# One decoder step on one Trainium2 core: feed-forward's first group in one 512-column matmul from inner block four, and two small products of linear attention on all 128 rows

## The chip, the core and the metric

The kernel runs on one core of a Trainium2 chip. The core has a matrix engine (TensorE, PE in the profile, with its weight loads as PEld), three engines for everything else (VectorE = DVE, ScalarE = ACT, GpSimd = POOL), and queues that issue transfers (SP's above all). TensorE writes to PSUM, eight banks of 512 fp32 columns on each of 128 partitions; the other engines read results there. The metric is device time in microseconds, the median of three runs.

## The reference

One step of a two-layer decoder: 512 prompt tokens and 8 sampled tokens, width 1024. Layer 0 mixes tokens with sliding-window attention, layer 1 with gated linear attention (GLA); behind each mixer stands a gated convolutional feed-forward of inner width 2816. Cut to what matters here:

```
def conv_ffn(x, buf, w_up, conv_w, conv_b, w_down):
    h = x @ w_up
    a, u = h[..., :D_FF], h[..., D_FF:]
    ap = concatenate([buf, a], axis=1)
    c = conv_b + sum(conv_w[j] * ap[:, j:j + T] for j in range(3))
    y = (gelu(c) * u) @ w_down
    return y, ap[:, T:]

def gla_mix(...):
    q, k, v, g = split(x @ w_in)
    log_a = log_sigmoid((x @ w_a1) @ w_a2 + b_a) / 16
    o, s_new = gla_recurrence(q, k, v, log_a, s0, chunk)
    ...
x = layer_norm(ALPHA * x + mixer(x)); x = layer_norm(ALPHA * x + conv_ffn(x))
```

All of it is float32.

## The kernel before

Tokens stand in the columns, features in the 128 rows (`P`), in eight blocks (`KD`). The 520 columns are two groups: a (256 prompt tokens) and b (256 prompt tokens and the 8 samples, 264 columns). The program is a list of units, one per block of 128 output features; each unit has one weight block of up to 1024 x 128 and runs first for group a and four or five units later for group b (`order`, with `LEADS` and `LAG`), so that a's results have time to become b's inputs. Feed-forward has 22 inner blocks j, in three parts of 6, 8 and 8 (`FF_PARTS`): for each j a gate unit (L530) and a value unit (L556), and after a part eight down units (L569) that add the part's products to x.

Precision: a weight block is split into a high part `wh` (rounded to the matmul's fp32r type, by ScalarE, L149) and a low part `wl` (what is left, by VectorE, L152); activations likewise into `xh`, `xl` (the normalised x) and `hh`, `hl` (the inner products). `product` (L155) sums, for each of a unit's k-steps, high x high, high x low and low x high in one bank: L164, L165, L166, three matmuls of 256 columns (group b: 264). The tiles of a group hold even and odd columns in two halves, and a matmul reads them in turn (`in_turn`), one column from each half.

Each matmul loads its own 128 x 128 weights. There are four accumulators (`accp`), six weight buffers (`WSLOTS`; one more in feed-forward, `EXTRA`) and two buffers for raw weights. What comes out of a gate product is copied with its two left neighbours (L540), goes through three convolution steps (L543 to L545) and GELU (L552); a value product is multiplied with it (L560) and split (L170, L171). Down products are added to x (L573, L575), or for the last part go into the layer norm.

In GLA the decay comes from a rank-16 product whose result `z` holds its rows in two halves; `gla_decay` (L633) multiplies one half, 64 rows, with `wa2` for each head and group. The samples' output (L784) gets its last term from a product with 8 rows, one per sample (`qkd`, `vsamp`). These two are plain fp32 matmuls.

Which instruction stands where on an engine is decided by the library's scheduler, which simulates the program; the engines then run their instructions in that order.

Of the kernel before, what the change touches and what calls it, by code (L numbers as in the profile page):

```python
# [11 lines left out]
F32 = mybir.dt.float32  # L12
# [8 lines left out]
P = 128  # L21
# [32 lines left out]
NSUB = 5  # L54

SPAUSE = 2
SPAUSEL = 3
# [19 lines left out]
def in_turn(rows):  # L77

    return rows.rearrange("p t j -> p j t")
# [10 lines left out]
class Net:  # L90
    def __init__(self, tc, ctx, I, O):
# [17 lines left out]
        nc.gpsimd.memset(self.ones_a, 1.0 / D)  # L109
        self.ones_c = c.tile([P, P], F32, name="ones_c")  # L110
        nc.gpsimd.memset(self.ones_c, 1.0 / P)
# [3 lines left out]
        for g in self.groups:  # L115
            s = [P, KD, g.n]
            g.x = self.act.tile(s, F32, name=f"x_{g.name}")

            s = [P, KD, 2, g.n // 2]
            g.xh = self.act.tile(s, F32R, name=f"xh_{g.name}")  # L120
# [34 lines left out]
    def product(self, g, u, rh, rl):  # L155
# [11 lines left out]
        return ps[:, :g.n]  # L167

    def split(self, hi, lo, src):
        self.nc.scalar.activation(hi, src, AF.Copy)  # L170
        self.nc.vector.tensor_tensor(lo, src, hi.bitcast(F32), op=ALU.subtract)  # L171
# [8 lines left out]
    def ln_chunk(self, g, m, ps, scaled, last=False):  # L180
# [11 lines left out]
        if m == 0:  # L192
            yield 1
            mp = self.mtile("sc")[:, :n]
            nc.tensor.matmul(mp, self.ones_c, x[:, 0], start=True, stop=True)
            sb = c("sb")
            nc.scalar.copy(sb, mp)
            sa = sb
            if not scaled:
                sa = c("sa")  # L200
                nc.scalar.activation(sa, mp, AF.Copy, scale=1.0 / ALPHA)
# [80 lines left out]
    def attn_open(self):  # L282
# [10 lines left out]
        for _ in range(WARM):  # L293
            nc.tensor.matmul(warm[:, :P], self.ones_c, self.ones_c, start=True, stop=True)
        with self.tc.manual_schedule(engines={mybir.EngineType.SP}):
# [234 lines left out]
    def ffn_gate(self, g, u, layer, j, q):  # L530
        nc, n = self.nc, g.n
        ps = self.product(g, u, g.xh, g.xl)
        w = lambda i: self.par[:, C_CW + (layer * 3 + i) * NF + j:C_CW + (layer * 3 + i) * NF + j + 1]
# [8 lines left out]
        c = t("conv")  # L542
        nc.scalar.activation(c[:, :256], ps[:, :256], AF.Identity, scale=w(2), bias=cb)  # L543
        nc.vector.scalar_tensor_tensor(c[:, :256], a[:, 1:257], w(1), c[:, :256], op0=ALU.mult, op1=ALU.add)
# [11 lines left out]
    def ffn_value(self, g, u, layer, j, q):  # L556
        nc, n = self.nc, g.n
        ps = self.product(g, u, g.xh, g.xl)
        h = self.fp.tile([P, NT - 256], F32, name="hprod", bufs=2)
        nc.vector.tensor_tensor(h[:, :n], g.gate[:, :n], ps, op=ALU.mult)  # L560
        self.split(g.hh[:, q], g.hl[:, q], parted(h[:, :n]))
# [7 lines left out]
    def ffn_down(self, g, u, layer, part, m):  # L569
        nc = self.nc  # L570
        ps = self.product(g, u, g.hh, g.hl)
        if part == 0:
# [60 lines left out]
    def gla_decay(self, g, h):  # L633
        nc, n = self.nc, g.n
        zp = self.mtile("sc")[:, :n]
        half = slice(64 * (h // 2), 64 * (h // 2) + 64)
        nc.tensor.matmul(zp, self.wa2[half, h % 2 * P:(h % 2 + 1) * P], g.z[half], start=True, stop=True)
        ba = self.par[:, C_BA + h:C_BA + h + 1]
# [122 lines left out]
    def gla_sample(self, g, h, q, k, v0, v1, ep, kraw):  # L761
# [10 lines left out]
        nc.tensor.matmul(mp[:NS, 256:257], pr, self.eps[:, 1:2], start=True, stop=True)  # L772
        vs = self.gp.tile([NS, 257], F32, name="vsamp")
        nc.vector.tensor_copy(vs, mp[:NS, :257])
        dv = self.dram.tile([NS, 256], F32, name="dv")
        nc.sync.dma_start(out=dv, in_=vs[:, :256])
        nc.vector.tensor_scalar(self.qkd.rearrange("p (j s) -> p s j", j=4)[:, 0:2],
                                self.ident[:NS, :NS].rearrange("p (t j) -> p t j", t=2), vs[:, 256:257], None, op0=ALU.mult)
        yield 1
# [209 lines left out]
def _layout(inp):  # L989
# [21 lines left out]
    a["w_a1"] = f["gla_w_a1"][0].reshape(KD, P, 16).transpose(1, 0, 2)  # L1011
    w2 = np.zeros((P, 256), np.float32)
    for i in range(2):
        w2[64 * i:64 * i + 16] = w2[64 * i + 32:64 * i + 48] = f["gla_w_a2"][0][:, 256 * i:256 * i + 256]
    a["w_a2"] = w2
# [42 lines left out]
```

## Time and profile before

| | us |
|---|---|
| median of three runs | 1170.98 (1170.62 to 1171.20) |
| the profiled execution | 1171.17 |
| its span, first to last instruction | 1169.5 |
| VectorE busy | 765.3 (65%) |
| ScalarE busy | 548.3 (47%) |
| HBM read and written | 108.54 MB and 8.47 MB |

The profile's page gives busy time by engine, the chain that ended last, and groups of instructions by line with their count, busy time, mean duration and the idle time ahead of them with what ended it. Views of the trace narrow this to a stretch, a line or a tile. In the rows, `accp<-xh_a,wh` names the tile written and the tiles read; `128*128` are the rows and columns of the weights, `128x256` the rows and columns of the moving operand. In the timeline the first number is the start and the second the duration; fp32 products show two records each (`x2`).

### The profile page before, as it was taken

The page shows a single profiled execution, that of the slowest core. Times are in us where ns is not written, and L with a number is a line of the kernel's source. Part 1 is how long each engine was busy: PE and PEld are TensorE (multiplying, and loading weights), DVE is VectorE, ACT ScalarE, POOL GpSimd, SP SyncE. Part 2 cuts the span into 40 slices and gives each one's busy share as a digit, 9 for nine tenths or more (in the row PEclk, how much of TensorE's full clock was granted, in tenths as well). Part 3 has the DMA queues.
Part 4 walks back from the last instruction along what each step waited for, and adds up shares of the span by engine and source line. Part 5 has one row for each costly group of instructions (what it writes and reads, how often), then busy time and mean ns, then how long its engine had stood idle before and what let it go on. Part 6 is the DMA issues. An engine that isn't in the chain of part 4 may idle for free.

```text
span 1169.5 us, 24320 instructions
## 1 busy us (share of the span) xinstructions
PE 1120.0 (96%) x9606; PEld 1086.6 (93%) x9606; DVE 765.3 (65%) x1575; ACT 548.3 (47%) x1192; POOL 362.5 (31%) x597
## 2 busy tenths in 40 slices
PE   8889898999999999999899999998999999999995
PEld 7888788999999999998799899898999999999995
DVE  7988869744555355468767787789645554455566
ACT  4456546533453234435545555456533453244433
POOL 5777767310111001156400100368200111011344
PEclk9999989999999999999899999999999999999998
DMA  7322022224322323233034354442323333323222
GB/s 231 114 90 74 2 79 91 83 82 127 99 100 94 106 91 109 73 125 120 26 93 124 128 189 140 142 132 73 98 86 125 104 97 94 106 92 108 74 62 73
DMA packets 48674, 118.59 MB, mean 101 GB/s; under 512 B 5768, under 2 KB 22320, under 8 KB 48560
## 3 DMA queue, kind: packets, MB, share of 16 engines
q1 hardware_dynamic: 46544, 115.41, 31.6%
q10 hardware_dynamic: 2016, 1.62, 0.4%
q8 instruction: 76, 1.25, 0.4%
q14 instruction: 38, 0.31, 0.1%
HBM read 108.54 MB, written 8.47 MB: 100 GB/s over the span
## 4 chain that ended last, share of the span: by engine, by line
PE 74%; DVE 14%; POOL 4%; issue 4%; DMA 2%; ACT 2%; SPq 0%; ACTq 0%; DVEq 0%; POOLq 0%
PE accp L165 23%; PE accp L164 23%; PE accp L166 23%; DVE wl L152 3%; DMA vb<-dv 2%; DVE qs L387 1%; POOL x_b L270 1%; POOL x_a L270 1%; DVE u L268 1%; DVE rb L338 1%; PE pv L460 1%; DVE msq L248 1%; PE sc L723 1%; DVE small L427 1%; DVE rb L336 1%
## 5 line engine op out<-in xcount | busy, mean ns | idle before, releaser
L152 DVE TENSOR_TENSOR wl<-raw,wh 128x1024 fp32r<-128x1024 f32 (+2 forms) x189 | 230.5, 1220 | 133.6 <-ACT wh L149 131.8
L149 ACT ACTIVATE wh<-raw 128x1024 fp32r<-128x1024 f32 (+1 forms) x176 | 183.2, 1041 | 216.4 <-PE accp L165 192.2
L164 PE MATMUL accp<-xh_b,wh 128*128 128x264 f32 x976 | 272.8, 280 | 2.7 <-DVE hprod L560 2.7
L164 PE MATMUL accp<-xh_a,wh 128*128 128x256 f32 x976 | 270.8, 280 | 4.2 <-DVE x_b L189 1.1
L165 PE MATMUL accp<-xl_a,wh 128*128 128x256 f32 x976 | 271.0, 279 | 3.3 <-DVE xl_a L273 2.9
L166 PE MATMUL accp<-xh_a,wl 128*128 128x256 f32 x976 | 270.8, 278 | 3.0 <-DVE wl L152 3.0
L165 PE MATMUL accp<-xl_b,wh 128*128 128x264 f32 x976 | 272.3, 279 | 0.2
L166 PE MATMUL accp<-xh_b,wl 128*128 128x264 f32 x976 | 271.6, 278 | 0.0
L164 PEld LDWEIGHTS accp<-xh_a,wh 128*128 128x128 f32 x976 | 187.4, 193 | 7.3 <-DVE x_b L189 1.6
L166 PEld LDWEIGHTS accp<-xh_a,wl 128*128 128x128 f32 x976 | 188.4, 193 | 4.9 <-DVE wl L152 4.0
L165 PEld LDWEIGHTS accp<-xl_a,wh 128*128 128x128 f32 x976 | 188.2, 193 | 5.0 <-DVE xl_a L273 3.6
L164 PEld LDWEIGHTS accp<-xh_b,wh 128*128 128x128 f32 x976 | 186.1, 191 | 4.0 <-DVE hprod L560 3.0
L165 PEld LDWEIGHTS accp<-xl_b,wh 128*128 128x128 f32 x976 | 186.1, 191 | 1.5 <-issue 0.7
L166 PEld LDWEIGHTS accp<-xh_b,wl 128*128 128x128 f32 x976 | 185.8, 190 | 0.8 <-issue 0.7
L164 PE MATMUL accp<-hh_b,wh 128*128 128x264 f32 x480 | 134.3, 280 | 3.0 <-ACT hh_b L170 3.0
L165 PE MATMUL accp<-hl_b,wh 128*128 128x264 f32 x480 | 134.6, 280 | 0.0
L166 PE MATMUL accp<-hh_b,wl 128*128 128x264 f32 x480 | 133.7, 278 | 0.0
L165 PE MATMUL accp<-hl_a,wh 128*128 128x256 f32 x480 | 132.2, 276 | 0.9 <-DVE hl_a L171 0.9
L164 PE MATMUL accp<-hh_a,wh 128*128 128x256 f32 x480 | 132.1, 278 | 0.0
L166 PE MATMUL accp<-hh_a,wl 128*128 128x256 f32 x480 | 131.9, 276 | 0.0
L164 PEld LDWEIGHTS accp<-hh_b,wh 128*128 128x128 f32 x480 | 91.7, 191 | 3.5 <-ACT hh_b L170 3.3
L165 PEld LDWEIGHTS accp<-hl_a,wh 128*128 128x128 f32 x480 | 92.0, 192 | 1.9 <-DVE hl_a L171 1.4
(306 smaller groups left out, 2052.8 us busy)
## 6 DMA issues: line engine op xcount, KB each, us to landing
raw<-in_w_up SPq DMA_DIRECT2D x88, 512.0 KB, 3.4
raw<-in_w_down SPq DMA_DIRECT2D x32, 512.0 KB, 3.5
raw<-in_w_gla SPq DMA_DIRECT2D x24, 512.0 KB, 3.4
raw<-in_w_mix_o SPq DMA_DIRECT2D x16, 512.0 KB, 3.4
raw<-in_w_down SPq DMA_DIRECT2D x16, 384.0 KB, 3.1
sgla<-in_state_gla SPq DMA_DIRECT2D x16, 256.0 KB, 2.8
vb<-dv SPq DMA_DIRECT2D x16, 256.0 KB, 3.9
out_gla_s<-sgla SPq DMA_DIRECT2D x16, 256.0 KB, 2.8
```

What stands on the lines that cost most here:

```text
L149: nc.scalar.activation(h[:, c], r[:, c], AF.Copy)
L152: nc.vector.tensor_tensor(l[:, c], r[:, c], h[:, c].bitcast(F32), op=ALU.subtract)
L164: nc.tensor.matmul(o, h[:, ks], xh, start=k == 0, stop=False)
L165: nc.tensor.matmul(o, h[:, ks], xl, start=False, stop=False)
L166: nc.tensor.matmul(o, l[:, ks], xh, start=False, stop=k == nt - 1)
L248: nc.vector.scalar_tensor_tensor(q, q, 0.5, nv, op0=ALU.mult, op1=ALU.mult)
L268: nc.vector.tensor_tensor(u, x[:, m], r, op=ALU.mult)
L270: ts = nc.gpsimd.tensor_scalar(x[:, m], u, sc(m), bi(m), op0=ALU.mult, op1=ALU.add)
L336: nc.vector.stream_shuffle(b, a, [(i + 16) % 32 for i in range(32)])
L338: nc.vector.tensor_tensor(b, b, tab[:, 1], op=ALU.mult)
L387: nc.vector.tensor_tensor(qs[oth, v], r[own, :256], qs[own, v].bitcast(F32), op=ALU.subtract)
L427: nc.vector.tensor_reduce(nm, sc[:, :, 0:P + 1], axis=AX.X, op=ALU.max, negate=True)
```

## The change

Group a's high and low parts are put side by side in one tile (`xs`, `hs`), and `xh`, `xl`, `hh`, `hl` become views of it. A new `product2` then multiplies the high weights with both parts in one matmul of 512 columns, and the low weights with the high part in one of 256, so that high x low lands in the upper half of the bank. It is used for gate and value from j = 4 (`WIDE`) on, which is the fifth block, and for the down products of parts 0 and 1. The two halves of the bank are added behind it: a gate on VectorE after the copy, a value by a ScalarE copy and a VectorE addition, a down product by a second addition to x. Group b and all other products stay as they are.

In GLA `wa2` is laid out as 128 rows per head, with zeros where the other half stands, and the samples' tiles get 128 rows, zero from row 8 on. The constant 1/128 is dropped: the layer norm's first mean uses the 1/1024 one and a scale of 8.

```
@@ __init__
+            if i == 0:
+                s = [P, KD, 2, 2, g.n // 2]
+                g.xs = self.act.tile(s, F32R, name=f"xs_{g.name}")
+                g.hs = self.act.tile(s, F32R, name=f"hs_{g.name}")
+                g.xh, g.xl = (g.xs[:, :, :, q] for q in range(2))
+                g.hh, g.hl = (g.hs[:, :, :, q] for q in range(2))
+                continue
+    def product2(self, g, u, rs, rh, rl, wide):
+        if rs is None or not wide:
+            return self.product(g, u, rh, rl), None
...
+        o = ps.rearrange("p (j t) -> p j t", t=2)
+        for k in range(nt):
+            ks = slice(k * P, (k + 1) * P)
+            last = k == nt - 1
+            both = lambda: nc.tensor.matmul(o, h[:, ks], in_turn(rs[:, k].rearrange("p t q j -> p t (q j)")), start=k == 0, stop=last)
+            low = lambda: nc.tensor.matmul(o[:, :P], l[:, ks], in_turn(rh[:, k]), start=False, stop=False)
+            for f in (low, both) if last else (both, low):
+                f()
+        return ps[:, :256], ps[:, 256:]
@@ ln_chunk
-            nc.tensor.matmul(mp, self.ones_c, x[:, 0], start=True, stop=True)
+            nc.tensor.matmul(mp, self.ones_a, x[:, 0], start=True, stop=True)
-            nc.scalar.copy(sb, mp)
+            nc.scalar.activation(sb, mp, AF.Copy, scale=float(KD))
@@ ffn_gate
-        ps = self.product(g, u, g.xh, g.xl)
+        ps, lo = self.product2(g, u, g.xs, g.xh, g.xl, j >= WIDE)
...
-        nc.scalar.activation(c[:, :256], ps[:, :256], AF.Identity, scale=w(2), bias=cb)
+        if lo is not None:
+            nc.vector.tensor_tensor(a[:, 2:2 + n], a[:, 2:2 + n], lo, op=ALU.add)
+        nc.scalar.activation(c[:, :256], ps[:, :256] if lo is None else a[:, 2:258], AF.Identity, scale=w(2), bias=cb)
@@ ffn_value
-        ps = self.product(g, u, g.xh, g.xl)
+        ps, lo = self.product2(g, u, g.xs, g.xh, g.xl, j >= WIDE)
+        if lo is not None:
+            nc.scalar.copy(h[:, :n], lo)
+            nc.vector.tensor_tensor(h[:, :n], h[:, :n], ps, op=ALU.add)
+            ps = h[:, :n]
@@ ffn_down
-        ps = self.product(g, u, g.hh, g.hl)
+        ps, lo = self.product2(g, u, g.hs, g.hh, g.hl, part < 2)
...
+        if lo is not None:
+            nc.vector.tensor_tensor(g.x[:, m], g.x[:, m], lo, op=ALU.add)
@@ gla_open, gla_decay, gla_sample
-        self.qkd = t([NS, P], "qkd")
+        self.qkd = t([P, P], "qkd")
+        self.vs = t([P, 257], "vsamp")
+        nc.gpsimd.memset(self.vs, 0.0)
-        self.wa2 = t([P, 256], "wa2")
+        self.wa2 = t([P, GH * P], "wa2")
-        half = slice(64 * (h // 2), 64 * (h // 2) + 64)
-        nc.tensor.matmul(zp, self.wa2[half, h % 2 * P:(h % 2 + 1) * P], g.z[half], start=True, stop=True)
+        nc.tensor.matmul(zp, self.wa2[:, h * P:(h + 1) * P], g.z, start=True, stop=True)
```

On TensorE, before the change, the last two k-steps of the first down product of part 0 in layer 0 (group a, six k-steps), and what follows it, a product of group b:

```order
L164 MATMUL accp<-hh_a,wh 128x256
L165 MATMUL accp<-hl_a,wh 128x256
L166 MATMUL accp<-hh_a,wl 128x256
L164 MATMUL accp<-hh_a,wh 128x256
L165 MATMUL accp<-hl_a,wh 128x256
L166 MATMUL accp<-hh_a,wl 128x256
L164 MATMUL accp<-xh_b,wh 128x264
L165 MATMUL accp<-xl_b,wh 128x264
```

And after, its last three k-steps (`hs_a` holds both parts):

```order
L191 MATMUL accp<-hs_a,wh 128x512
L192 MATMUL accp<-hs_a,wl 128x256
L191 MATMUL accp<-hs_a,wh 128x512
L192 MATMUL accp<-hs_a,wl 128x256
L173 MATMUL accp<-xh_b,wh 128x264
L174 MATMUL accp<-xl_b,wh 128x264
L175 MATMUL accp<-xh_b,wl 128x264
L192 MATMUL accp<-hs_a,wl 128x256
L173 MATMUL accp<-xh_b,wh 128x264
L174 MATMUL accp<-xl_b,wh 128x264
L175 MATMUL accp<-xh_b,wl 128x264
L191 MATMUL accp<-hs_a,wh 128x512
```

Two matmuls per k-step stand where three did. Before, the product ran in one piece; now three matmuls of the next product of group b stand ahead of each of the two of its last k-step, whose input is the last to be ready.

On VectorE, before, from a gate of group a to the end of the value that follows it, at the same place of the program (`wl` is the next weights' low part; the 8-column operation is group b's gate):

```order
L544 SCALAR_TENSOR_TENSOR conv<-aext,par,conv 128x256
L545 SCALAR_TENSOR_TENSOR conv<-aext,par,conv 128x256
L152 TENSOR_TENSOR wl<-raw,wh 128x768
L549 SCALAR_TENSOR_TENSOR conv<-aext,par,base 128x8
L544 SCALAR_TENSOR_TENSOR conv<-aext,par,conv 128x256
L545 SCALAR_TENSOR_TENSOR conv<-aext,par,conv 128x256
L560 TENSOR_TENSOR hprod<-conv,accp 128x256
L171 TENSOR_TENSOR hl_a<-hprod,hh_a 128x256
```

And after:

```order
L572 TENSOR_TENSOR aext<-aext,accp 128x256
L574 SCALAR_TENSOR_TENSOR conv<-aext,par,conv 128x256
L575 SCALAR_TENSOR_TENSOR conv<-aext,par,conv 128x256
L161 TENSOR_TENSOR wl<-raw,wh 128x768
L579 SCALAR_TENSOR_TENSOR conv<-aext,par,base 128x8
L574 SCALAR_TENSOR_TENSOR conv<-aext,par,conv 128x256
L575 SCALAR_TENSOR_TENSOR conv<-aext,par,conv 128x256
L592 TENSOR_TENSOR hprod<-hprod,accp 128x256
L594 TENSOR_TENSOR hprod<-conv,hprod 128x256
L199 TENSOR_TENSOR hs_a<-hprod,hs_a 128x2x128
```

Two additions have come in (L572, L592); the rest stands as it did.

On ScalarE, late in part 2 of a layer, a gate and a value of each group before the change (`wh` is the next weights' high part):

```order
L540 COPY aext<-accp 128x256
L543 ACTIVATE conv<-accp,par 128x256
L552 ACTIVATE conv<-conv 128x256
L149 ACTIVATE wh<-raw 128x1024
L540 COPY aext<-accp 128x264
L543 ACTIVATE conv<-accp,par 128x256
L170 ACTIVATE hh_a<-hprod 128x256
L552 ACTIVATE conv<-conv 128x264
```

And after:

```order
L568 COPY aext<-accp 128x256
L573 ACTIVATE conv<-aext,par 128x256
L158 ACTIVATE wh<-raw 128x1024
L582 ACTIVATE conv<-conv 128x256
L568 COPY aext<-accp 128x264
L573 ACTIVATE conv<-accp,par 128x256
L591 COPY hprod<-accp 128x256
L582 ACTIVATE conv<-conv 128x264
L198 ACTIVATE hs_a<-hprod 128x2x128
```

The weights' copy has moved ahead of group a's GELU (L582), and a copy of the upper half of the value's bank has come in (L591).

More of the change, by code (lines that the diff above doesn't have):

```diff
@@ L54 @@
 NSUB = 5
+WIDE = 4
 SPAUSE = 2
@@ L109, in __init__ @@
         nc.gpsimd.memset(self.ones_a, 1.0 / D)
-        self.ones_c = c.tile([P, P], F32, name="ones_c")
-        nc.gpsimd.memset(self.ones_c, 1.0 / P)
         self.eps = c.tile([P, 2], F32, name="eps")
@@ L114, in __init__ @@
         nc.gpsimd.memset(self.eps[:, 1:2], 1.0)
-        for g in self.groups:
+        for i, g in enumerate(self.groups):
             s = [P, KD, g.n]
             g.x = self.act.tile(s, F32, name=f"x_{g.name}")
+            if i == 0:
[5 more added lines that the diff above has]
+                continue
             s = [P, KD, 2, g.n // 2]
+            g.xs = g.hs = None
             g.xh = self.act.tile(s, F32R, name=f"xh_{g.name}")
@@ L167, in product @@
         return ps[:, :g.n]
+    def product2(self, g, u, rs, rh, rl, wide):
+        if rs is None or not wide:
+            return self.product(g, u, rh, rl), None
+        nc = self.nc
+        h, l = self.w[u]
+        nt = self.units[u][1]
+        ps = self.acc.tile([P, 512], F32, name="accp")
+        o = ps.rearrange("p (j t) -> p j t", t=2)
[7 more added lines that the diff above has]
+        return ps[:, :256], ps[:, 256:]
     def split(self, hi, lo, src):
@@ L200, in ln_chunk @@
                 sa = c("sa")
-                nc.scalar.activation(sa, mp, AF.Copy, scale=1.0 / ALPHA)
+                nc.scalar.activation(sa, mp, AF.Copy, scale=KD / ALPHA)
             for i in range(KD):
@@ L293, in attn_open @@
         for _ in range(WARM):
-            nc.tensor.matmul(warm[:, :P], self.ones_c, self.ones_c, start=True, stop=True)
+            nc.tensor.matmul(warm[:, :P], self.ones_a, self.ones_a, start=True, stop=True)
         with self.tc.manual_schedule(engines={mybir.EngineType.SP}):
@@ L772, in gla_sample @@
         nc.tensor.matmul(mp[:NS, 256:257], pr, self.eps[:, 1:2], start=True, stop=True)
-        vs = self.gp.tile([NS, 257], F32, name="vsamp")
-        nc.vector.tensor_copy(vs, mp[:NS, :257])
+        vs = self.vs
+        nc.vector.tensor_copy(vs[:NS], mp[:NS, :257])
         dv = self.dram.tile([NS, 256], F32, name="dv")
-        nc.sync.dma_start(out=dv, in_=vs[:, :256])
-        nc.vector.tensor_scalar(self.qkd.rearrange("p (j s) -> p s j", j=4)[:, 0:2],
-                                self.ident[:NS, :NS].rearrange("p (t j) -> p t j", t=2), vs[:, 256:257], None, op0=ALU.mult)
+        nc.sync.dma_start(out=dv, in_=vs[:NS, :256])
+        nc.vector.tensor_scalar(self.qkd[:NS].rearrange("p (j s) -> p s j", j=4)[:, 0:2],
+                                self.ident[:NS, :NS].rearrange("p (t j) -> p t j", t=2), vs[:NS, 256:257], None, op0=ALU.mult)
         yield 1
@@ L1011, in _layout @@
     a["w_a1"] = f["gla_w_a1"][0].reshape(KD, P, 16).transpose(1, 0, 2)
-    w2 = np.zeros((P, 256), np.float32)
-    for i in range(2):
-        w2[64 * i:64 * i + 16] = w2[64 * i + 32:64 * i + 48] = f["gla_w_a2"][0][:, 256 * i:256 * i + 256]
+    w2 = np.zeros((P, GH * P), np.float32)
+    for h in range(GH):
+        o = 64 * (h // 2)
+        w2[o:o + 16, h * P:(h + 1) * P] = w2[o + 32:o + 48, h * P:(h + 1) * P] = f["gla_w_a2"][0][:, h * P:(h + 1) * P]
     a["w_a2"] = w2
```

## The prediction

> **What bounds the kernel now.** I read the page first: the busy lines and the chain.
>
> ```profile
> span 1169.5 us, 24320 instructions
> PE 1120.0 (96%) x9606; PEld 1086.6 (93%) x9606; DVE 765.3 (65%) x1575; ACT 548.3 (47%) x1192; POOL 362.5 (31%) x597
> ...
> PE 74%; DVE 14%; POOL 4%; issue 4%; DMA 2%; ACT 2%; SPq 0%; ACTq 0%; DVEq 0%; POOLq 0%
> ```
>
> TensorE is busy 96% of the span and carries 74% of the chain that ends last. Such an average mixes stages, so the second view is busy time by stretches: feed-forward of layer 0 (212 to 540), the way into linear attention (540 to 575), linear attention (575 to 760), feed-forward of layer 1 (820 to 1100).
>
> ```profile
> core 0: us, PE busy (x) PEld busy (x) DVE busy (x) ACT busy (x) POOL busy (x), PEclk, DMA share, GB/s
> ...
> 212.00:465.00 253.00, 253.00 (x2259) 253.00 (x2259) 131.27 (x236) 104.59 (x186) 30.60 (x86) 1.00 0.32 101
> 465.00:540.00 75.00, 75.00 (x664) 74.78 (x663) 46.45 (x82) 32.75 (x62) 31.25 (x48) 1.00 0.34 106
> 540.00:575.00 35.00, 29.36 (x212) 25.81 (x210) 31.98 (x70) 19.13 (x37) 23.14 (x22) 0.93 0.18 61
> 575.00:760.00 185.00, 183.36 (x1497) 170.06 (x1496) 135.23 (x323) 95.38 (x247) 20.04 (x26) 0.99 0.42 132
> ...
> 820.00:1100.00 280.00, 280.00 (x2501) 280.00 (x2500) 145.65 (x263) 117.27 (x210) 34.46 (x97) 1.00 0.33 101
> ```
>
> In the feed-forward stretches TensorE has no idle time at all (253.00 of 253.00, 280.00 of 280.00, clock 1.00) while VectorE is at 52% and ScalarE at 41%. So there every nanosecond taken from the matmul stream shortens the span by as much, and work added on the other two is free as long as it makes TensorE wait for nothing. Linear attention is nearly so: 183.36 of 185.
>
> A matmul's row says 0.28 us, but matmuls overlap; what it costs is the distance to the next one's start. The third view is the timeline of TensorE in a quiet place.
>
> ```profile
> 400.34 0.28 PE L164 MATMUL accp<-hh_b,wh 128*128 128x264 f32 x1
> ...
> 403.05 0.27 PE L164 MATMUL accp<-xh_a,wh 128*128 128x256 f32 x1
> ...
> 405.72 0.28 PE L164 MATMUL accp<-hh_b,wh 128*128 128x264 f32 x1
> ```
>
> From 400.34 to 403.05 stand 24 matmuls of group b (264 columns): 0.113 us each. From 403.05 to 405.72 stand 24 of group a (256 columns): 0.111 each. One k-step of group a (three matmuls) is thus 0.334 us. Eight columns fewer save only 0.002 of 0.113, where columns alone would save 0.003, so a 256-column matmul holds a few nanoseconds that are not columns.
>
> **Part 1: wide products in the feed-forward.** From inner block j = 4 on, gate and value of group a, and the down-products of parts 0 and 1, run two matmuls per k-step instead of three: one of 512 columns (high and low part side by side) on the high weights, one of 256 on the low weights. Count: 18 blocks x 2 products x 8 k-steps x 2 layers = 576, and (6 + 8) k-steps x 8 outputs x 2 layers = 224: 800 of group a's 1456 k-steps (976 + 480, the counts of the rows of L164). The trace has no 512-column matmul of this kind. The nearest are the full fp32 products of linear attention, which have two records per instruction; the rows below also hold the decay and sample products, for part 2.
>
> ```profile
> 613.22 0.28 PE L165 MATMUL accp<-xl_b,wh 128*128 128x264 f32 x1
> 613.33 0.59 PE L731 MATMUL pv<-sp,q_b 128*128 128x256 f32 x2
> 613.76 0.59 PE L734 MATMUL pv<-vk,attm 128*128 128x256 f32 x2
> 614.01 0.46 PE L166 MATMUL accp<-xh_b,wl 128*128 128x264 f32 x1
> 614.31 0.28 PE L164 MATMUL accp<-xh_b,wh 128*128 128x264 f32 x1
> ...
> 614.98 0.28 PE L164 MATMUL accp<-xh_b,wh 128*128 128x264 f32 x1
> 615.19 0.69 PE L784 MATMUL sc<-vsamp,qkd 8*128 8x256 f32 x2
> 615.81 0.38 PE L165 MATMUL accp<-xl_b,wh 128*128 128x264 f32 x1
> 616.03 0.28 PE L166 MATMUL accp<-xh_b,wl 128*128 128x264 f32 x1
> ```
>
> ```profile
> 616.93 0.27 PE L707 MATMUL tp<-ident,v_a 128*128 128x128 f32 x1
> 617.04 0.27 PE L708 MATMUL tp<-ident,v_a 128*128 128x128 f32 x1
> 617.24 0.70 PE L637 MATMUL sc<-z_a,wa 64*128 64x256 f32 x2
> 617.86 0.38 PE L164 MATMUL accp<-xh_a,wh 128*128 128x256 f32 x1
> 618.08 0.28 PE L165 MATMUL accp<-xl_a,wh 128*128 128x256 f32 x1
> ```
>
> A 128-column fp32 record costs 0.11 (616.93 to 617.04), about a 256-column matmul of the stream, so an fp32 column counts as two. The two records of L731 take 613.33 to 613.76, 0.215 each: that is my price for 512 columns. Its upper bound is 2 x 0.111 = 0.222 (every column as dear as now: gain nil). Its lower bound lies with the matmul beside it: if the 256-column one also went at 0.109, the pair would be 0.324. I take 0.216 + 0.111 = 0.327, since the fp32 row is the only one whose stream is as long. Gain: 800 x (0.334 - 0.327) = **5.6 us** (0 to 8.0).
>
> Beside it come, for group a (the first row is the weight subtraction that shares VectorE's queue), a VectorE addition per product (18 x 2 x 2 + 16 x 2 = 104) and a ScalarE copy per value product (36).
>
> ```profile
> L152 DVE TENSOR_TENSOR wl<-raw,wh 128x1024 fp32r<-128x1024 f32 (+2 forms) x189 | 230.5, 1220 | 133.6 <-ACT wh L149 131.8
> ```
>
> ```profile
> L560 DVE TENSOR_TENSOR hprod<-conv,accp 128x256 f32<-128x256 f32 x44 | 18.4, 418 | 3.7 <-PE accp L166 3.7
> ...
> L540 ACT COPY aext<-accp 128x256 f32<-128x256 f32 x44 | 16.3, 371 | 56.5 <-PE accp L166 56.5
> ...
> L575 DVE TENSOR_TENSOR x_a<-x_a,accp 128x256 f32<-128x256 f32 x16 | 6.7, 421 | 3.5 <-PE accp L166 2.7
> ...
> L170 ACT ACTIVATE hh_a<-hprod 128x256 fp32r<-128x256 f32 x44 | 19.8, 450 | 58.6 <-DVE hprod L560 58.6
> L171 DVE TENSOR_TENSOR hl_a<-hprod,hh_a 128x256 fp32r<-128x256 f32 x44 | 19.2, 437 | 9.5 <-ACT hh_a L170 6.4
> ```
>
> 104 x 0.42 = 44 us more on VectorE and 36 x 0.37 = 13 us on ScalarE, over about 600 us: VectorE goes from 52% to some 59% there. I cost them at nothing, the cover being TensorE's full stream. Three places could break it. (a) The accumulator: four buffers, and a product is 2.7 us (24 x 0.111), so a buffer is wanted back some 8 us after its product ends; it is held about 0.4 us longer. (b) The last value product before the down-products: copy, addition, multiplication, split and rest are 0.37 + 0.42 + 0.42 + 0.45 + 0.44 = 2.1 us, against 1.3 now. The block that it writes is the last k-step of the first down-product, and ahead of it TensorE has a whole product of group b (2.7) and five k-steps (1.6): 4.3 us. Even behind one weight subtraction of 1.22 us in VectorE's queue the chain ends in time. (c) Weights: the order puts the weights' copy ahead of the gate's GELU. What that copy waits for is this:
>
> ```profile
> L149 ACT ACTIVATE wh<-raw 128x1024 fp32r<-128x1024 f32 (+1 forms) x176 | 183.2, 1041 | 216.4 <-PE accp L165 192.2
> ```
>
> ScalarE stands there until TensorE frees a weight buffer, so the copy starts when group b's product ends, now as before. The GELU behind it then ends some 1.5 us after that end, and its value product needs another 2.6 us to finish. No new wait. The other edits there (a scaled copy in place of a copy, one constant less, group a's tiles laid out together) add no instruction; whether the new layout is read as fast is a rival below.
>
> **Part 2: decay and sample products on 128 rows.** Eight decay products (L637, 64 rows) and four sample products (L784, 8 rows) get all 128. From 617.04 to 618.08 are 1.04 us; less one transpose (0.11) and one matmul (0.11), the decay product costs 0.82. The sample product costs the same: 614.98 to 616.03 less two matmuls, 0.82. Two full-row products (L731, L734) cost 614.31 - 613.22 less two matmuls (0.226) = 0.864, or 0.43 each. The saving is 0.39 each. Full rows are no guess here: L731 and L734 are of the same type and width. Bounds: 0 if the excess is not from the rows, 0.39. The first decay product saves nothing, because TensorE waits for group b's normalised rows soon after anyway:
>
> ```profile
> 565.04 0.28 PE L166 MATMUL accp<-xh_a,wl 128*128 128x256 f32 x1
> 566.16 0.38 PE L626 MATMUL accp<-xh_b,wh 128*128 128x264 f32 x1 [0.85 <-ACT v_a L695]
> ```
>
> So 11 x 0.39 = **4.3 us** (0 to 4.7). The Trainium skill says of this, on the page "TensorE: Matmul & The Clock Gate", section "Why this matters for your kernels", that a single matmul on 32 rows takes as long as one on 128. By it this part would save nothing; the trace disagrees, 0.82 against 0.43.
>
> **Sum.** The profiled execution took 1171.17 us (span 1169.5), 0.19 above the median of 1170.98. 1171.17 - 5.6 - 4.3 = 1161.3, and at the median **1161.1**, 0.85% less.
>
> **Rivals.**
> 1. *The 256-column matmul of the pair also goes at its stream's pace* (0.109, the lower bound above): gain 8.0, time 1158.7. For it: after the change its successor's weights are no longer followed by another short matmul on each side. Against: the weight load for the next long matmul still has only this short one to hide behind. The Trainium skill, same page, section "Back-to-back issue gap", gives 2.5 ns per matmul beside its columns at 2.4 GHz, that is 109.2 and 215.8 ns here; the trace has 113 for 264 columns as it says, but 111 for 256, not 109.
> 2. *The gain of part 1 does not arrive*: 512 columns cost twice 256, or a new wait eats it. The wait would be (b): six changes of part at up to 1.3 us each (0.8 more chain and some queue) are 7.8, more than the 5.6. Time 1166.7. Against it is the margin of 4.3 against 2.1 us.
> 3. *Partial rows are not what makes part 2 slow*, but the change from one matmul type to another: 1165.4. Against: L731 has the same neighbours and none of the excess.
> 4. *Slower: the new layout is read more slowly.* Group a's columns are fetched alternately from two halves, 128 elements apart before and 256 now, in every product of group a, wide or not. That the order of reading has a price is seen at the scores, whose moving rows are contiguous:
>
> ```profile
> 47.17 0.28 PE L164 MATMUL accp<-xh_a,wh 128*128 128x256 f32 x1
> 47.28 0.28 PE L412 MATMUL sc<-khi,qs 128*128 128x256 f32 x1
> 47.40 0.28 PE L413 MATMUL sc<-klo,qs 128*128 128x256 f32 x1
> 47.52 0.28 PE L412 MATMUL sc<-khi,qs 128*128 128x256 f32 x1
> ```
>
> 0.12 each instead of 0.111. With 0.009 on each of 3 x 1456 = 4368 stretches of 256 columns, 39 us come on top, less the 9.9 of the sum: some 1200. It decides from 9.9 / 4368 = 2.3 ns per 256 columns. Against: group b alternates at 132 elements and shows no excess over group a, so the distance does not seem to matter.
>
> Beside these the granted clock moves: 0.93 over the 35 us from 540 to 575 is 2.5 us lost. One such spell more or less is worth that much either way.
>
> **How the numbers follow.** Forecast (1161.1, itself 1159 to 1163.5 with the clock): 0.70. Rival 1: 0.10. Rival 2: 0.11. Rival 3: 0.03. Rival 4: 0.06. The range runs from rival 1 with some of the clock, 1157.5, to just under rival 2, 1166.5: about 0.83 inside. The measurement can tell about 0.2% (2.3 us) from no change. Slower by more: 0.06, rival 4. Within it: 0.03, rival 2 with both mechanisms at once. Faster: 0.91.
>
> **What would show it.** Part 1: in a quiet stretch, starts of the wide pair 0.216 and 0.111 apart, TensorE still without idle time, group b unchanged at 0.113. 0.222 or 0.109 would speak for rival 2 or 1. Rival 4 would show in the not wide products of group a, above 0.113 already in layer 0's attention. Part 2: decay and sample products at 0.43. Waits of TensorE for `hs_a` at a change of part, or for the weights, would show the cover broken. The prediction is wrong if the long matmul is not near 0.216, or if stages that the change does not touch move by more than the clock explains.

## The result and the profile after

The kernel after takes 1159.55 us (median of four runs, 1154.76 to 1161.33) beside 1170.8 for the kernel before (1169.93 to 1171.2): ratio 0.9898, 95% interval 0.9866 to 0.9931. Two more sets of runs of the same program gave medians of 1160.95 and 1161.17. The forecast was 1161.1. The ratios in this document leave out two executions that took far longer than their fellows, one of the kernel before (1185.06 us) and one of g_fill (2391.95 us).

The page of the kernel after: span, busy time, and the engines' shares of the chain that ended last.

```profile
span 1153.0 us, 22833 instructions
...
PE 1102.3 (96%) x8806; PEld 1052.4 (91%) x8806; DVE 809.6 (70%) x1679; ACT 565.2 (49%) x1228; POOL 348.0 (30%) x597
...
PE 74%; DVE 14%; POOL 4%; issue 3%; DMA 2%; ACT 2%; SPq 0%; ACTq 0%; DVEq 0%; POOLq 0%
```

TensorE has 800 matmuls fewer and is still busy for 96%. VectorE has 104 operations and 44 us more. That the shares hardly move shows that they cannot tell what an edit is worth; the stretches can. Of the same kernel, busy time by stretch:

```profile
212.00:465.00 253.00, 253.00 (x1911) 243.22 (x1911) 153.16 (x286) 113.11 (x203) 22.81 (x85) 1.00 0.32 103
...
540.00:575.00 35.00, 28.60 (x222) 26.30 (x221) 30.91 (x71) 21.61 (x44) 22.18 (x22) 1.00 0.19 61
575.00:760.00 185.00, 184.06 (x1546) 175.00 (x1545) 141.54 (x330) 96.93 (x250) 25.86 (x33) 1.00 0.44 140
820.00:1100.00 280.00, 280.00 (x2133) 269.63 (x2133) 167.46 (x310) 124.15 (x224) 33.77 (x101) 1.00 0.30 97
```

In the feed-forward TensorE is still without a gap (253.00 of 253.00, 280.00 of 280.00), now with VectorE at 60% and ScalarE at 45%. The weight loads, whose column was as full as TensorE's before, have air now: 243.22 of 253. The clock from 540 to 575 us is 1.00, where it was 0.93.

TensorE's timeline in a quiet place, inside a wide product:

```profile
394.77 0.38 PE L191 MATMUL accp<-hs_a,wh 128*128 128x512 f32 x1
394.99 0.27 PE L192 MATMUL accp<-hs_a,wl 128*128 128x256 f32 x1
395.10 0.38 PE L191 MATMUL accp<-hs_a,wh 128*128 128x512 f32 x1
...
396.08 0.38 PE L191 MATMUL accp<-hs_a,wh 128*128 128x512 f32 x1
```

From 394.77 to 396.08 stand four pairs: 0.3275 us each, where three matmuls took 0.334. Within the pair the long one takes 0.218 and the short one 0.109 (means of 340 to 460 us).

The decay product and the sample product with 128 rows, same view:

```profile
607.05 0.28 PE L173 MATMUL accp<-xh_b,wh 128*128 128x264 f32 x1
607.17 0.59 PE L822 MATMUL sc<-vsamp,qkd 128*128 128x256 f32 x2
...
607.71 0.28 PE L175 MATMUL accp<-xh_b,wl 128*128 128x264 f32 x1
...
653.22 0.27 PE L746 MATMUL tp<-ident,v_a 128*128 128x128 f32 x1
653.32 0.60 PE L675 MATMUL sc<-z_a,wa 128*128 128x256 f32 x2
...
653.87 0.28 PE L174 MATMUL accp<-xs_a,wh 128*128 128x256 f32 x1
```

Read as in the prediction: 607.71 - 607.05 less two matmuls (0.225), and 653.87 - 653.22 less a transpose and a matmul (0.22), both 0.43, where 0.82 stood.

### The profile page after: what moved, and what is told of

Its sections match the earlier page's. It is cut to its first block, busy times and chain, and to the rows that moved or that the text cites. A ratio compares the mean times of both kernels' runs of the same rounds, so it can differ in the third digit from the quotient of the medians.

```text
span 1153.0 us, 22833 instructions
## 1 busy us (share of the span) xinstructions
PE 1102.3 (96%) x8806; PEld 1052.4 (91%) x8806; DVE 809.6 (70%) x1679; ACT 565.2 (49%) x1228; POOL 348.0 (30%) x597
## 4 chain that ended last, share of the span: by engine, by line
PE 74%; DVE 14%; POOL 4%; issue 3%; DMA 2%; ACT 2%; SPq 0%; ACTq 0%; DVEq 0%; POOLq 0%
PE accp L174 15%; PE accp L191 15%; PE accp L175 15%; PE accp L173 15%; PE accp L192 8%; DVE wl L161 2%; DMA vb<-dv 1%; POOL x_b L298 1%; DVE qs L415 1%; POOL x_a L298 1%; DVE u L296 1%; PE pv L488 1%; DVE msq L276 1%; PE sc L761 1%; DVE rb L366 1%
## 5 line engine op out<-in xcount | busy, mean ns | idle before, releaser
L191 PE MATMUL accp<-xs_a,wh 128*128 128x512 f32 x576 | 196.3, 382 | 0.0
L192 PE MATMUL accp<-xs_a,wl 128*128 128x256 f32 x576 | 145.4, 273 | 0.0
L191 PEld LDWEIGHTS accp<-xs_a,wh 128*128 128x128 f32 x576 | 109.2, 190 | 11.3
L173 PE MATMUL accp<-xs_a,wh 128*128 128x256 f32 x400 | 111.4, 284 | 5.7 <-DVE x_b L219 2.1
L174 PE MATMUL accp<-xs_a,wh 128*128 128x256 f32 x400 | 111.4, 281 | 3.4 <-DVE xs_a L301 2.7
L175 PE MATMUL accp<-xs_a,wl 128*128 128x256 f32 x400 | 111.1, 280 | 3.0 <-DVE wl L161 3.0
L192 PEld LDWEIGHTS accp<-xs_a,wl 128*128 128x128 f32 x576 | 110.3, 191 | 1.9
L202 POOL COPY hist<-aext 128x2 f32<-128x2 f32 x44 | 8.9, 202 | 284.7 <-DVE aext L572 281.6
L174 PEld LDWEIGHTS accp<-hl_b,wh 128*128 128x128 f32 x480 | 91.6, 191 | 1.4 <-issue 0.3
L175 PEld LDWEIGHTS accp<-hh_b,wl 128*128 128x128 f32 x480 | 91.5, 191 | 0.2
```

The costliest lines, as they stand in the source:

```text
L173: nc.tensor.matmul(o, h[:, ks], xh, start=k == 0, stop=False)
L174: nc.tensor.matmul(o, h[:, ks], xl, start=False, stop=False)
L175: nc.tensor.matmul(o, l[:, ks], xh, start=False, stop=k == nt - 1)
L191: both = lambda: nc.tensor.matmul(o, h[:, ks], in_turn(rs[:, k].rearrange("p t q j -> p t (q j)")), start=k == 0, stop=last)
L192: low = lambda: nc.tensor.matmul(o[:, :P], l[:, ks], in_turn(rh[:, k]), start=False, stop=False)
```

## The experiments

Ten further kernels ran, and the kernel after ran twice more (d_again, j_after). Ratios are to the kernel before on the same chip, with 95% intervals. The line numbers in a run's rows are its own.

### The two parts alone, the layout alone, and the whole again

**a_rows**: the kernel before with part 2 alone, and the constant dropped.

```
-        self.qkd = t([NS, P], "qkd")
+        self.qkd = t([P, P], "qkd")
...
-        self.wa2 = t([P, 256], "wa2")
+        self.wa2 = t([P, GH * P], "wa2")
...
-        nc.tensor.matmul(zp, self.wa2[half, h % 2 * P:(h % 2 + 1) * P], g.z[half], start=True, stop=True)
+        nc.tensor.matmul(zp, self.wa2[:, h * P:(h + 1) * P], g.z, start=True, stop=True)
```

> Part 2 alone (decay and sample products on 128 rows, the constant 1/128 dropped; no wide product, old layout). Theory 1 (two independent gains, 5.6 us of wide pairs and 4.3 us of full rows; what is left over in the times is the granted clock): 4.3 us under the kernel before at the same granted clock, 0.43 us for each of the twelve products. Theory 2 (the gain beyond the wide pairs comes from shifted waits, not from the rows): 0 to 1 us under. Theory 3 (the change itself rids the core of its half-rate spells): a clock as before, 0.986, since the feed-forward is untouched.

**b_wide**: the kernel after with the decay and sample products as they were before (the edit above, undone).

> Part 1 alone (wide products and the new layout; decay and sample products on 64 and 8 rows as before). Theory 1: 5.6 us under the kernel before at the same clock, the decay product back at 0.82 us. Theory 2: 10 us under. Theory 3: the clock rises to 0.99 and the time falls by 8 us or more.

**c_layout**: the kernel before with the new layout and the dropped constant, and no wide product.

```
+WIDE = NF
...
+            if i == 0:
+                s = [P, KD, 2, 2, g.n // 2]
+                g.xs = self.act.tile(s, F32R, name=f"xs_{g.name}")
```

> The new layout alone (high and low part of group a side by side, every product with three matmuls, old decay and sample products, the constant 1/128 dropped). Theory 1: no difference from before, a 256-column matmul of group a at 0.1115 us. Rival 4 of the prediction (the distance of 256 columns is read more slowly or faster): another distance between the starts, 0.1 us of time for every 0.023 ns.

**d_again**: the kernel after, once more.

> The changed kernel once more, for its granted clock. Theory 1 (spells of half rate come and go by chance of phase): among these runs clocks of about 0.986 with 1161 us and higher clocks with shorter times, some 1.2 us per 0.001 of clock. Theory 3 (the change rids the core of the spells): most runs at 0.990 or above and under 1157 us, and the kernel before never.

| | median, us | ratio to before |
|---|---|---|
| before (17 runs) | 1169.88 | |
| a_rows | 1165.08 | 0.9957 (0.9945 to 0.9968) |
| b_wide | 1165.67 | 0.9961 (0.9946 to 0.9977) |
| c_layout | 1169.45 | 0.9999 (0.9988 to 1.0009) |
| d_again | 1160.95 | 0.9919 (0.9906 to 0.9932) |

By the ratios part 2 is worth 5.0 us (3.7 to 6.4) and part 1 4.6 (2.7 to 6.3). Their sum of 9.6 is what the whole gives, 9.5 (8.0 to 11.0): within the noise the two add up. The runs of a_rows had a little more clock than those of before (0.988 to 0.991, mean 0.990, beside 0.985 to 0.992, mean 0.988), so up to 2 us of its 5.0 may be the clock's (0.002 of 1170); b_wide had none more. The layout is worth nothing that these runs can tell, either way. Group a's quiet stretch in c_layout, where every matmul reads the new layout:

```profile
403.47 0.27 PE L173 MATMUL accp<-xs_a,wh 128*128 128x256 f32 x1
...
404.47 0.28 PE L173 MATMUL accp<-xs_a,wh 128*128 128x256 f32 x1
```

Nine matmuls in 1.00 us are 0.111 each, as in the old layout. Rival 4, the slower read, falls.

Where the 0.39 us of a product on few rows go can be seen in the weight loads of the kernel before, at its decay product (64 rows):

```profile
617.24 0.29 PEld L637 LDWEIGHTS sc<-z_a,wa 64*128 64x128 f32 x2 [0.17 <-issue]
617.86 0.19 PEld L164 LDWEIGHTS accp<-xh_a,wh 128*128 128x128 f32 x1 [0.33 <-issue]
```

The queue of the loads stands idle ahead of this product (0.17 us) and behind it (0.33 us), as it does at all twelve; in the kernel after the idle times there are 0.03 us or less. Otherwise a load starts ahead of its own matmul, beneath the one before; this one starts with its own, at 617.24.

### What the 111 ns of a short matmul are

**e_cols**: the kernel before, one of group a's three matmuls per k-step cut to 192 columns.

```
-            nc.tensor.matmul(o, h[:, ks], xl, start=False, stop=False)
+            cut = g.n // 2 if g.i else 96
+            nc.tensor.matmul(o[:, :cut], h[:, ks], xl[:, :cut], start=False, stop=False)
```

> The kernel of before, with group a's high x low matmul cut from 256 to 192 columns (64 of its columns of that term are left out of the computation). It asks what the 111.6 ns of a 256-column matmul are. Theory floor: a matmul cannot be followed sooner than the next matmul's weights are loaded, some 109 to 112 ns; then a shorter matmul changes nothing: from the start of the cut one to the next start stay 109 to 112 ns in the quiet stretch from 340 to 460 us, and the time stays within 3 us of before. Then the pair of the change gains because its long matmul covers a load and its short one no longer has a load of equal length on both sides. Theory columns: time goes with columns plus a constant; then the cut one takes three quarters, 80 to 87 ns, and with more than 1456 such matmuls the time falls by 36 us or more.

Measured: 1169.47 us in a single run, beside a median of 1169.8 for before (17 runs, 1167.28 to 1173.8). A twelfth of group a's columns is gone, and no time with it that can be told. TensorE's timeline of e_cols, from the first of five k-steps of group a to the one behind them:

```profile
400.61 0.27 PE L164 MATMUL accp<-xh_a,wh 128*128 128x256 f32 x1
400.72 0.25 PE L166 MATMUL accp<-xl_a,wh 128*128 128x192 f32 x1
400.81 0.30 PE L167 MATMUL accp<-xh_a,wl 128*128 128x256 f32 x1
400.94 0.28 PE L164 MATMUL accp<-xh_a,wh 128*128 128x256 f32 x1
...
402.29 0.28 PE L164 MATMUL accp<-xh_a,wh 128*128 128x256 f32 x1
```

And its weight loads (PEld) in the same stretch:

```profile
400.62 0.19 PEld L166 LDWEIGHTS accp<-xl_a,wh 128*128 128x128 f32 x1
400.73 0.19 PEld L167 LDWEIGHTS accp<-xh_a,wl 128*128 128x128 f32 x1
...
401.95 0.19 PEld L166 LDWEIGHTS accp<-xl_a,wh 128*128 128x128 f32 x1
```

The cut matmul is followed after 0.085 (mean of 340 to 460 us), as the column theory says; the one behind it is then followed late, after 0.138. Five k-steps still take 1.68 us; the mean of one is 0.335. The loads tell why: twelve of them from 400.62 to 401.95, 0.111 each, evenly, whatever the matmuls between them do. My expectation named the wrong distance (it wanted 109 to 112 ns behind the cut matmul itself), but the theory behind it holds: **the stream of the kernel before went at the pace of its weight loads**, one per matmul, not of its columns. The long and the short matmul of a pair differ by 218 - 109 = 109 ns for 256 columns, so the columns of a k-step need about 3 x 109 = 327 ns, its three loads 3 x 111.6 = 335. The pair has the same columns and two loads: it runs at the pace of its columns. That is where the 7 ns come from.

Every matmul of the stream has a load, so a fixed cost of each matmul would look the same. Two other places of the kernel before tell them apart:

```profile
143.35 1.38 PE L492 MATMUL pv<-pts,vc 128*128 128x16 f32 x11
...
739.81 0.19 PE L772 MATMUL tp<-eps,qk 128*8 128x1 f32 x2
739.93 0.70 PE L723 MATMUL sc<-vk 128*128 128x256 f32 x2
```

The eleven matmuls at 143.35 move only 16 columns each, but load weights of 128 columns: they start 0.112 apart. The two at 739.81 load weights of 8 columns, and the next product starts 0.12 after the first of them, for both. The pace goes with the columns of the weights; a fixed cost of 0.11 for each matmul does not fit.

The Trainium skill (page "TensorE: Matmul & The Clock Gate", section "LDWEIGHTS (loading the stationary operand)") gives the time of a load as its columns divided by 1.2, in ns; an estimate from that is 106.7 for 128 columns. The loads of this trace stand 111.6 apart (the mean of group a's in the kernel before, 340 to 460 us), a little more. By that rule the floor could have been looked for before the run.

### How much cover is left

**h_cover**: the kernel after with two VectorE additions that nobody needs, ahead of each wide gate's and value's own.

```
+    def idle(self, lo):
+        for _ in range(2):
+            self.nc.vector.tensor_tensor(self.junk, self.junk, lo, op=ALU.add)
...
+            self.idle(lo)
```

> The kernel after, with two more VectorE additions on a scratch tile ahead of each wide gate and value product's own addition: 72 products, 144 operations of 0.42 us, 60 us more on VectorE, and 0.84 us more on each chain. It asks how much cover the change left. Theory 1 (TensorE's full stream hides it: margin 4.3 us against a chain of 2.1, now 2.9): the time stays within 1.5 us of the kernel after, TensorE busy for all of 230 to 460 us. Rival 2 (the change's own additions already use the cover up): waits of TensorE for hs_a or for weights appear in the feed-forward stretches, and the time rises by 3 us or more, ratio to before above 0.993.

Measured: 1159.85 us, ratio 0.9915 (0.9892 to 0.9937). Its feed-forward stretches:

```profile
212.00:465.00 253.00, 253.00 (x1916) 243.31 (x1916) 174.73 (x350) 112.23 (x204) 29.73 (x87) 1.00 0.32 103
820.00:1100.00 280.00, 280.00 (x2126) 269.39 (x2125) 192.60 (x384) 124.15 (x226) 37.72 (x100) 1.00 0.30 98
```

VectorE has 22 and 25 us more than in the kernel after, and TensorE waits for none of it; from 465 to 540 us it is busy for 75.00 of 75.00 too, so it waits at no change of part. The scheduler ordered this kernel anew, around the added work. The cover was not close to used up; rival 2's wait at a change of part falls with some room.

### More wide products

**f_all**: the wide pair everywhere in group a's feed-forward.

```
-WIDE = 4
+WIDE = 0
...
-        ps, lo = self.product2(g, u, g.hs, g.hh, g.hl, part < 2)
+        ps, lo = self.product2(g, u, g.hs, g.hh, g.hl, True)
...
+            if lo is not None:
+                nc.vector.tensor_tensor(g.x[:, m], g.x[:, m], lo, op=ALU.add)
+                lo = None
```

> The kernel after, with the wide pair in all of group a's feed-forward products: blocks 0 to 3 too and the down products of part 2, whose upper half is added to x ahead of the layer norm. 128 + 128 = 256 more wide k-steps. Theory 1 (the 7.0 ns per k-step hold wherever TensorE is full): 1.8 us less than the kernel after, some 1158 to 1159, ratio to before 0.990. Rival (the longer chain in the layer norm at a layer's end is waited for): 256 x 7.0 ns are eaten, in the bound 8 x 0.42 us for each of two layers are added: 1160 to 1167, and waits of TensorE for xs_a or the layer norm's operands grow behind the last down product.

Measured: 1164.56 us, ratio 0.9952 (0.9933 to 0.9971): some 4 us lost against the kernel after (1160.95 in d_again), in place of 1.8 gained. Its timeline at the start of layer 0's feed-forward (in brackets the idle time and what ended it):

```profile
181.86 0.45 PE L191 MATMUL accp<-xs_a,wh 128*128 128x512 f32 x1 [1.72 <-DVE xs_a L301]
...
199.10 0.48 PE L191 MATMUL accp<-xs_a,wh 128*128 128x512 f32 x1 [3.37 <-DVE aext L572]
```

The kernel after at the same place:

```profile
179.86 0.39 PE L173 MATMUL accp<-xs_a,wh 128*128 128x256 f32 x2
181.26 0.38 PE L174 MATMUL accp<-xs_a,wh 128*128 128x256 f32 x1 [1.01 <-DVE xs_a L301]
```

While the first inputs of a layer are still being normalised, short matmuls can run ahead with the high parts (two of them at 179.86); a wide one cannot start before VectorE has written the low part too, and waits 1.72 us. And the longer life of an accumulator, free of charge in full swing, is waited for here: 3.37 us, ended by the addition of a gate's two halves. At the first gates of both layers together TensorE waits 11.1 us in f_all and 8.7 in the kernel after. Another share is likely the clock's: in f_all's profiled execution it falls to half at 183.1 and at 200.1 us, for 3.4 us each, where it does in no other. My rival had the time right and the place wrong, the end of a layer.

**f_down** takes the place apart: blocks 0 to 3 short again (`WIDE = 4`), part 2's down products still wide.

> The kernel after, with the down products of part 2 wide as well, blocks 0 to 3 left as they are: 8 outputs x 8 k-steps x 2 layers = 128 more wide k-steps. The run with all products wide lost some 4 us against the kernel after, and its trace has the longer waits at the first gates of a layer (180 to 199 and 784 to 805 us), where a wide matmul cannot start before the low part is there. Theory first gates: with blocks 0 to 3 narrow again the loss goes, 128 x 7.0 ns = 0.9 us less than the kernel after, 1158 to 1160, ratio to before 0.990 to 0.991. Rival (the addition ahead of the layer norm costs too): 1161 to 1165, with longer waits of TensorE behind the last down product at 540 to 575 us.

Measured: 1159.14 us, ratio 0.9909 (0.9894 to 0.9924). The loss is gone; it lay at the first gates. Whether the 0.9 us of the 128 wide k-steps are there cannot be told from these medians.

### The clock

The kernel after ran from 1154.8 to 1162.4 us in its three sets, the one program. Its profiled execution (1154.76) and that of d_again (1161.57) differ by 6.8 us. Granted clock by windows (the number after POOL's), first the kernel before:

```profile
40.00:47.00 7.00, 6.87 (x46) 6.87 (x47) 6.77 (x15) 4.50 (x17) 5.00 (x6) 0.76 0.32 94
...
147.00:153.50 6.50, 5.99 (x33) 5.43 (x34) 1.67 (x5) 1.42 (x5) 2.40 (x7) 0.50 0.10 30
564.00:577.00 13.00, 9.98 (x47) 7.72 (x47) 9.22 (x25) 8.46 (x18) 6.24 (x6) 0.74 0.07 16
782.00:797.00 15.00, 12.62 (x94) 12.10 (x93) 15.00 (x28) 8.46 (x14) 12.09 (x11) 0.89 0.37 125
```

then d_again:

```profile
40.00:47.00 7.00, 6.79 (x46) 6.79 (x46) 6.77 (x15) 4.48 (x18) 5.08 (x6) 0.76 0.30 94
...
564.00:577.00 13.00, 11.12 (x58) 9.74 (x59) 8.38 (x23) 7.20 (x15) 2.87 (x4) 0.74 0.12 41
782.00:797.00 15.00, 13.02 (x95) 12.71 (x96) 14.64 (x30) 10.07 (x17) 13.46 (x10) 0.89 0.41 139
```

and the profiled execution of the kernel after:

```profile
40.00:47.00 7.00, 6.01 (x48) 5.61 (x48) 6.80 (x18) 4.35 (x16) 5.14 (x6) 1.00 0.28 88
...
145.00:154.00 9.00, 6.66 (x40) 5.90 (x40) 2.21 (x7) 2.57 (x8) 4.77 (x12) 0.62 0.09 23
564.00:577.00 13.00, 11.03 (x78) 10.02 (x78) 10.56 (x27) 7.62 (x18) 2.14 (x3) 1.00 0.13 41
782.00:797.00 15.00, 14.61 (x123) 13.93 (x121) 14.55 (x28) 9.24 (x17) 13.54 (x15) 1.00 0.29 100
```

There are five places at which the clock falls to half for 3.4 or 6.8 us (near 41, 85, 147, 568 and 788 us), and every execution ends with 8 to 11 us at half. In the kernel before, TensorE was busy for 0.93 to 1.72 us of the 3.41 ahead of each of the five. Before and d_again show the spell at all five, the profiled execution of j_after (1159.99, see below) at three, that of the kernel after at one; there TensorE was busy for 2.16 of the 3.41 us ahead of it, with matmuls of 16 columns for the most part. So the change does not rid the kernel of these spells; one execution was luckier. Between the two with the same five spells the difference is 1171.17 - 1161.57 = 9.6 us, against a forecast of 9.9.

**g_fill** tries to keep the clock: matmuls whose result nobody reads, in three of TensorE's waits.

```
+    def fill(self, ps, rhs, n):
+        for _ in range(n):
+            mm = self.nc.tensor.matmul(ps, self.ones_a, rhs, start=True, stop=True)
...
+            self.fill(pv[:, 256:384], pt, 10)
...
+                    last = self.fill(bank, g.xh[:, k, 0, :P].bitcast(F32), 2)
```

> The kernel after, with fp32 matmuls whose result nobody reads put into three of TensorE's waits: ten behind the samples' attention product (the wait at 144 us), two between the k-steps of group b's rank-16 product (566 us), six behind the first matmul of layer 1's feed-forward (780 us). Theory clock (half-rate spells follow a stretch of 3.4 us in which TensorE streamed less than about 0.4 of the time): the spells at 146 (6.8 us long), 566 to 573 and 785 us go, each worth half its length; granted clock 0.990 or more in every run, the median 1153 to 1157, with less spread than the kernel after. Rival 1 (the spells come by something else than TensorE's idling): spells at the same places, 1159 to 1162. Rival 2 (the fillers stand in the way of real work): TensorE's waits shrink by less than the fillers take, 1160 to 1164 although the spells are gone.

Measured: 1168.19 us (median of twelve), ratio 0.9984 (0.9970 to 0.9997). None of the three forecasts came true: the fillers stand in the way as rival 2 says, but at a higher price, and in the profiled execution two of the three spells are still there, 6.8 us each at 147.9 and at 567.8. The timeline of g_fill at the rank-16 product:

```profile
564.63 0.28 PE L679 MATMUL accp<-xl_b,wh 128*128 128x264 f32 x1
569.99 1.22 PE L201 MATMUL accp<-xh_b,ones_a 128*128 128x128 f32 x4 [5.09 <-DVE q_a L725]
```

The filler's own bank was not free for 5.09 us, and in TensorE's queue everything stood behind it: a wait of that length ahead of the spell is the opposite of what the fillers were for. The ten at the samples' product wrote into the tile that the product's split reads, and TensorE still waited 3.0 us for `hh_b` behind them.

**g_fill2** gives the ten another bank and writes three into the bank that the rank-16 product then overwrites; the six in layer 1 stay.

```
-            self.fill(pv[:, 256:384], pt, 10)
+            self.fill(self.mtile("sc")[:, :P], pt, 10)
...
+        if g.i:
+            self.fill(ps[:, :P], g.xh[:, 0, 0, :P].bitcast(F32), 3)
```

> The fillers again, now where they hold up no real work: ten behind the samples' attention product in a bank of their own (in the first try the split of that product waited for them), three ahead of group b's rank-16 product in the bank that it then overwrites (in the first try their bank came free 5.4 us late), six behind the first matmul of layer 1's feed-forward as before. Theory clock: the spells at 146, 566 and 785 us go, granted clock 0.990 or more in most runs, median 1154 to 1158. Rival 1 (fillers do not keep the clock): spells at the same places, 1159 to 1162. Rival 2 (they still hold up real work, 4.2 us of them in all): 1160 to 1164 without the spells.

Measured: 1157.18 us (1155.61 to 1159.57), ratio 0.9903 (0.9887 to 0.9919), granted clock 0.992 to 0.995 in all five runs. Its windows at the three places:

```profile
145.00:154.00 9.00, 8.02 (x71) 7.12 (x71) 4.24 (x9) 3.75 (x9) 5.88 (x12) 1.00 0.13 32
564.00:577.00 13.00, 13.00 (x89) 12.40 (x89) 9.81 (x17) 5.54 (x13) 1.55 (x2) 0.87 0.21 67
782.00:797.00 15.00, 14.44 (x119) 13.90 (x120) 13.88 (x28) 8.94 (x17) 12.74 (x13) 1.00 0.33 107
```

The spell at 146, which every profiled execution without working fillers had, is gone. That there is none at 785 shows nothing, since a_rows, b_wide, c_layout, h_cover and j_after, without working fillers, have none there either; and the spells at 41 and 85, where no filler stands, were missing by luck, as in the kernel after. At 564 a spell of 3.4 us came in spite of the three fillers.

**i_both** joins g_fill2 and f_down, and **j_after** runs the kernel after beside it on the same chip.

> The kernel after, unchanged, beside the next one on the same chip: 1158 to 1161.5, granted clock 0.985 to 0.990 in most runs.

> The fillers of the second try and the wide down products of part 2 together. Theory: the gains add, 0.9 us from the down products and 2 to 4 us from the kept clock, 3 to 5 us less than the kernel after beside it, granted clock 0.992 or more. Rival (what the fillers gained before was another chip or the luck of the runs): within 2 us of the kernel after beside it.

Measured: j_after 1161.17 us (1159.83 to 1162.35), ratio 0.9930 (0.9914 to 0.9946); i_both 1157.00 (1155.98 to 1160.61), ratio 0.9897 (0.9880 to 0.9914). The 4.2 us between them are within the theory's 3 to 5, and above what the rival allows; five of the six runs of i_both lie below all six of j_after. The granted clock was 0.989 to 0.995 in i_both and 0.984 to 0.991 in j_after. The profiled execution of i_both has no spell at 147, 564 or 785, but two where no filler stands (41.8 and 86.2). What f_down's edit adds to the fillers is not shown: g_fill2 alone had 0.9903. By its median i_both is faster than the kernel before and the kernel after.

## Why the prediction was right, and where it was not

**The bound** was read rightly: in the feed-forward TensorE has no idle time before or after, and what was taken from its stream came off the span, as far as the noise lets it be told.

**Part 1, the sum**: 0.334 - 0.327 was forecast; as means from 340 to 460 us, 0.3348 before and 0.3275 after were measured. 800 times, that is 5.6 and 5.8 us. The part alone gave 4.6 (2.7 to 6.3).

**Part 1, its two prices**: both a little off, in opposite directions, and that the two errors cancel is luck. The long matmul takes 0.218, not 0.216 from the fp32 rows; the short one 0.109, not 0.111. Rival 1 had the short one right, and would have been the result had the long one been at 0.216. (Its pair of 0.324 takes the long one at 0.215, the forecast at 0.216: two roundings of one reading, worth 0.8 us in 800 pairs.) The prediction saw "a few nanoseconds that are not columns" in the short matmul and did not say what they are; e_cols and the two places beside it show that they are the load of the next weights, which binds only where the matmul is as short as the load. Against rival 1 stood that the load for the long matmul has only the short one to hide behind: it does, and the short one goes at 0.109 all the same, since a pair has 0.327 us for its two loads. The Trainium skill (page "TensorE: Matmul & The Clock Gate", section "Back-to-back issue gap") gives for a single matmul, at the full clock, its columns divided by 2.4 and 2.5 more, in ns; an estimate from that is 109.2 for 256 columns and 215.8 for 512. The trace agrees on the short one (109.3), and is 2 ns above it on the long one (218).

**The cover**: costed at nothing, and nothing it was; h_cover put about 47 us more on VectorE in the two stretches and found no wait. At a change of part the margin was read well. In the kernel after, the last value of part 0 in layer 0, from the copy out of its bank to the matmul that reads the block:

```profile
237.39 0.37 ACT L591 COPY hprod<-accp 128x256 f32<-128x256 f32 x1 [0.91 <-PE accp L191]
...
239.18 0.43 DVE L199 TENSOR_TENSOR hs_a<-hprod,hs_a 128x256 fp32r<-128x256 f32 x1 [0.50 <-ACT hs_a L198]
...
241.81 0.27 PE L192 MATMUL accp<-hs_a,wl 128*128 128x256 f32 x1
```

The chain takes 2.2 us and has 4.4, where 2.1 and 4.3 were forecast. The additions stand in the profile with the durations that were taken from other rows:

```profile
L572 DVE TENSOR_TENSOR aext<-aext,accp 128x256 f32<-128x256 f32 x36 | 15.2, 422 | 22.2 <-ACT aext L568 22.0
...
L615 DVE TENSOR_TENSOR x_a<-x_a,accp 128x256 f32<-128x256 f32 x32 | 13.4, 419 | 0.8
```

f_all shows where it would not have held: at the first blocks of a layer, which the change leaves alone.

**Part 2**: 0.82 to 0.43 for both products, as forecast; 11 x 0.39 = 4.3 us, and 5.0 (3.7 to 6.4) by the part alone, some of which may be the clock's. The rule of the Trainium skill that was weighed there (page "TensorE: Matmul & The Clock Gate", section "Why this matters for your kernels"), that a matmul on few rows takes as long as one on 128, would have saved nothing; in this kernel the partial rows cost 0.39 more, not the same. The trace shows where the time goes, to loads that do not run ahead; why they do not is not settled by these runs.

**Rivals 2, 3 and 4** fall by h_cover, a_rows and c_layout.

**The clock** is the term that was mis-sized. I allowed 2.5 us for one spell more or less; the number of spells moves by up to four. One program's executions lie 7.6 us apart (1154.76 to 1162.35), and two profiled ones, with one spell and with five, by 6.8. The median of 1159.55 is within the range, and the 1.5 us between it and the forecast are within that spread; they say nothing on the two parts.

## What to carry to other kernels

Where each matmul loads its own weights, look at the distance of the loads as well as of the matmuls: if the loads are evenly spaced and full, columns below the pace of the loads are free and loads are not, and the same columns in fewer matmuls are faster. Such a merge belongs where inputs lie ready and buffers are plenty; at a stage's start it delays the first matmul and holds a bank that is needed. Compare profiled executions with the same clock spells, and where waits cannot be removed, a few matmuls in them can be worth more than they cost, provided that their bank is free and nobody reads it.

## What was not expected of the hardware

Cutting 64 of 256 columns out of one matmul in three saved nothing (1169.47 against 1169.8 us), since the loads stood 0.111 us apart all the same. A product on 8 or 64 rows cost 0.82 us, the same on 128 rows with zeros 0.43. And the half-rate spells last 3.4 or 6.8 us, start at multiples of 3.41 us from one another within an execution (before: 41.1, 85.4, 146.9, 570.1 and 792.0 us by the trace's clock records, 13, 18, 124 and 65 steps apart), and come behind a step of 3.41 us in which TensorE was busy for 0.93 to 1.72 us. The Trainium skill (page "TensorE: Matmul & The Clock Gate", section "Part 1: The HAM clock gate") says that the clock is halved after an idle window, and that the windows are 3413 ns of a free-running grid. The grid agrees; the window need not be idle, since 0.93 to 1.72 us of work in it did not prevent the spell. From what share of work on the clock is kept was not measured.
